# Rotating 96 images by a quarter turn: where the first store stands against the last load

## Chip, cores and metric

The kernel runs on one core of one Trainium2 chip. The metric is the time of one execution on the device, in microseconds (us). The times given are the median of three runs, and one further look with the hardware profiler shows where each engine and the DMA queue spend that time. In the profile PE is TensorE, DVE is VectorE, ACT is ScalarE, POOL is GpSimd, and SP is SyncE, which here does nothing but issue DMAs.

## Reference

```python
def setup_inputs():
    batch, c, h, w = 32, 3, 256, 256
    return {"x": np.random.randn(batch, c, h, w).astype(np.float32)}

def reference(x: np.ndarray) -> np.ndarray:
    return np.rot90(x, k=-1, axes=(-2, -1)).astype(np.float32)
```

There are 32 x 3 = 96 images of 256 x 256 float32 values, 256 KB each. Every image is turned by 90 degrees clockwise. No arithmetic is done: 24 MB are read, rearranged inside each image and 24 MB are written.

## Kernel before

The input is cut into 12 slabs of 8 images, 2 MB each (`n_slabs` is 12, `last` is 11). A slab lies in one SBUF tile `units[n]` of 128 partitions by `I` = 2 halves of `F` = 2048 values, 8 KB per half and partition. All twelve tiles stand in SBUF at once, so no load waits for a tile to come free.

**Loads.** A first loop issues all 24 loads, two for each slab and 1 MB each, on the SP queue. The first and the last slab are loaded as 128 partitions by 8 KB (line 63), the other ten as 64 partitions by 16 KB, on every second partition (line 65).

**Turning.** A second loop over the slabs lets DVE turn one slab with two transposes of 128 x 2048 values (line 73 for the first and the last slab, line 79 for the others). The turned slab n is written into the tile of slab n - 1, which has been read by then. Slab 0 goes to a PSUM tile `turned0`. After the last slab, ACT copies `turned0` into `units[last]` (line 92).

**Stores.** Within the same second loop each turned slab is stored, also from the SP queue. Slab 1 goes out in three parts: 1 KB of each partition (128 KB, line 82), the other 7 KB of that half (896 KB, line 83), and the second half (1 MB, line 84). Slabs 2 and 3 go out in two halves of 1 MB (line 87), slabs 4 to 11 as whole 2 MB transfers (line 89), and slab 0 at the very end (line 93).

**What sets the order.** All 40 transfers are issued by SP in the order of the program, 24 loads and then 16 stores, and they drain one after another through one queue that is spread over 16 DMA engines. The framework hands out eight completion semaphores in turn, so SP issues a transfer only when the one eight places earlier has landed; a store also waits for the transposes that made its data. Stores therefore stand in the queue behind the last loads well before those have landed.

Of the kernel before, what the change touches and what calls it, by code (L numbers as in the profile page):

```python
# [1 line left out]

# [4 lines left out]

@with_exitstack
def kernel(
    ctx: ExitStack,
    tc: tile.TileContext,
    x: bass.AP,
    out: bass.AP,
):

    nc = tc.nc
    fp32 = mybir.dt.float32

    B, C, H, W = x.shape
    P = nc.NUM_PARTITIONS  # L40
    RI, RO = 16, 8
    K = H // RI
    I = 2
    Q = P // (K * I)
    n_slabs = B * C // (Q * I)
    last = n_slabs - 1
    F = RO * W

    rows_in = x.rearrange("b c h w -> (b c h) w")
    rows_out = out.rearrange("b c h w -> (b c h) w")  # L50
    ld8_v = rows_in.rearrange("(n i p r) w -> n p i (r w)", i=I, p=P, r=RO)
    ld16_v = rows_in.rearrange("(n i m r) w -> n i m (r w)", i=I, m=Q * K, r=RI)
    st_v = rows_out.rearrange("(n i p c) w -> n p i (c w)", i=I, p=P, c=RO)

    pools = [ctx.enter_context(tc.tile_pool(name=f"unit{u}", bufs=1)) for u in range(n_slabs)]
    units = [pool.tile([P, I, F], fp32, name=f"u{u}") for u, pool in enumerate(pools)]
    psum = ctx.enter_context(tc.tile_pool(name="psum", bufs=1, space=bass.MemoryType.PSUM))
    turned0 = psum.tile([P, I, F], fp32, name="turned0")

    for n in range(n_slabs):  # L60
        for i in range(I):
            if n in (0, last):
                nc.sync.dma_start(out=units[n][:, i], in_=ld8_v[n][:, i])
            else:
                nc.sync.dma_start(out=units[n][i::I].rearrange("p i f -> p (i f)"), in_=ld16_v[n, i])

    for n in range(n_slabs):
        t_in, t_out = units[n], units[n - 1] if n else turned0
        if n in (0, last):
            for i in range(I):  # L70
                src = t_in[:, i].rearrange("p (r g c) -> p c r g", r=RO, c=RO)
                dst = t_out[:, i].rearrange("p (c g r) -> p c r g", c=RO, r=RO)
                nc.vector.transpose(out=dst[:, :, ::-1, ::-1], in_=src)  # L73
        else:
            src = t_in.rearrange("p i f -> p (i f)").rearrange("p (r g c) -> p c r g", r=RI, c=RO)
            dst = t_out.rearrange("p i (c k r) -> p c r k i", c=RO, r=RI)[:, :, ::-1, ::-1, :]
            for h in range(2):
                cs = slice(h * RO // 2, (h + 1) * RO // 2)
                nc.vector.transpose(out=dst[:, cs], in_=src[:, cs])  # L79

        if n == 1:
            nc.sync.dma_start(out=st_v[n][:, 0, :W], in_=t_out[:, 0, :W])
            nc.sync.dma_start(out=st_v[n][:, 0, W:], in_=t_out[:, 0, W:])
            nc.sync.dma_start(out=st_v[n][:, 1], in_=t_out[:, 1])
        elif n in (2, 3):
            for i in range(I):
                nc.sync.dma_start(out=st_v[n][:, i], in_=t_out[:, i])
        elif n:
            nc.sync.dma_start(out=st_v[n], in_=t_out)

    for i in range(I):
        nc.scalar.copy(out=units[last][:, i], in_=turned0[:, i])  # L92
    nc.sync.dma_start(out=st_v[0], in_=units[last])


# [1 line left out]
_INS = ['x']  # L97
_OUTS = [((32, 3, 256, 256), 'float32')]


# [23 lines left out]
```

## Time and profile before

| | |
|---|---|
| Time, median of three runs | 123.94 us (123.78 to 124.06) |
| The profiled execution's own time | 124.06 us |
| Its span in the profile | 122.3 us |
| DVE busy | 93.3 us, 76% of the span, 24 transposes |
| ACT busy | 5.0 us |
| Moved by DMA | 50.33 MB, 25.17 read and 25.17 written, 412 GB/s over the span |
| DMA packets' time | 97.8% of 16 engines' span |

The span is the part of the execution that the profile covers; the 1.8 us by which the execution's own time is longer lie outside of it. A DMA issue on SP is short (a few tenths of a us) and says only when a transfer is put in the queue; "to landing" is the time from there until its completion semaphore is full. The rows of windows give, for a stretch of the span, the busy time of each engine and the rate at which DMA packets moved bytes.

### The profile page before, as it was taken

How to read it: one execution, taken by the hardware profiler on the slowest of the kernel's cores; microseconds unless marked ns; L12 is line 12 of the kernel's file. 1: busy time of each engine (PE TensorE's matmuls, PEld its weight loads, DVE VectorE, ACT ScalarE, POOL GpSimd, SP SyncE). 2: the span in 40 equal slices, each digit the busy share in tenths (PEclk: the TensorE clock that was granted, in tenths of full speed). 3: DMA queues.
4: the chain of work that ended last, by engine and by line, in shares of the span. 5: the costliest groups of instructions: out<-in, count | busy, mean ns of one | idle time of the engine just before them, and what ended most of it. 6: DMA issues, size and time to landing. Idle time of an engine off the chain costs nothing.

```text
span 122.3 us, 138 instructions
## 1 busy us (share of the span) xinstructions
DVE 93.3 (76%) x24; ACT 5.0 (4%) x3; POOL 0.2 (0%) x4
## 2 busy tenths in 40 slices
DVE  0199999999999999999999999999999940000000
ACT  0000000000000000000400000000000641000000
POOL 0000000000000000000000000000000000000000
DMA  3999999999999999999999999999999999999994
GB/s 118 418 450 429 429 429 429 429 429 429 429 429 429 429 429 429 429 429 391 359 413 429 429 429 426 429 421 429 429 429 429 429 429 429 429 429 426 429 429 180
DMA packets 5632, 50.33 MB, mean 412 GB/s; under 512 B 640, under 2 KB 768, under 8 KB 896
## 3 DMA queue, kind: packets, MB, share of 16 engines
q1 hardware_dynamic: 5632, 50.33, 97.8%
HBM read 25.17 MB, written 25.17 MB: 412 GB/s over the span
## 4 chain that ended last, share of the span: by engine, by line
DVE 47%; issue 27%; DMA 4%; DVEq 3%; ACT 2%
DVE u L79 37%; DVE turned L73 6%; DMA u<-in_x_dram 4%; DVE u L73 3%; DVEq L119 3%; ACT u L92 2%
## 5 line engine op out<-in xcount | busy, mean ns | idle before, releaser
L79 DVE STREAM_TRANSPOSE u<-u 128x2048 f32<-128x2048 f32 x20 | 78.0, 3949 | 0.3
L73 DVE STREAM_TRANSPOSE turned<-u 128x2048 f32<-128x2048 f32 x2 | 7.6, 3828 | 5.6 <-DMA u<-in_x_dram 5.6
L73 DVE STREAM_TRANSPOSE u<-u 128x2048 f32<-128x2048 f32 x2 | 7.7, 3953 | 0.0
L92 ACT COPY u<-turned 128x2048 f32<-128x2048 f32 x2 | 3.7, 1866 | 36.5 <-DVE u L73 36.5
L92 ACT ACT_TABLE_LOAD x1 | 1.3, 1283 | 59.7 <-DMA u<-in_x_dram 59.7
L108 POOL MEMSET const-bfloat16-1.0<- 128x1 bf16 x1 | 0.1, 102 | 0.0
L108 POOL MEMSET const-uint8-127<- 128x1 uint8 x1 | 0.1, 102 | 0.0
L108 POOL MEMSET const-float32-0.0<- 128x1 f32 x1 | 0.1, 99 | 0.2 <-issue 0.2
L108 POOL MEMSET const-float32-1.0<- 128x1 f32 x1 | 0.1, 99 | 0.0
## 6 DMA issues: line engine op xcount, KB each, us to landing
u<-in_x_dram SPq DMA_DIRECT2D x24, 1024.0 KB, 19.6
out_dram<-u SPq DMA_DIRECT2D x9, 2048.0 KB, 23.0
out_dram<-u SPq DMA_DIRECT2D x5, 1024.0 KB, 17.7
out_dram<-u SPq DMA_DIRECT2D x1, 896.0 KB, 17.8
out_dram<-u SPq DMA_DIRECT2D x1, 128.0 KB, 18.3
```

What stands on the lines that cost most here:

```text
L73: nc.vector.transpose(out=dst[:, :, ::-1, ::-1], in_=src)
L79: nc.vector.transpose(out=dst[:, cs], in_=src[:, cs])
L92: nc.scalar.copy(out=units[last][:, i], in_=turned0[:, i])
L108: nc = _bacc.Bacc("TRN2", target_bir_lowering=False, num_devices=1)
L119: with _tile.TileContext(nc) as tc:
```

## The change

`M` is 128 / 4 = 32. The last slab is loaded by three transfers in place of two: its first half as before, then 32 partitions of the second half (256 KB, called `near_end`), then the other 96 partitions (768 KB). The first store, 128 KB of slab 1, gets a dependency on `near_end`, so SP does not issue it until `near_end` has landed, and all later stores stand behind it on SP. Slabs 2 and 3 are stored as whole 2 MB transfers, like slabs 4 to 11. The transposes, the copies and the other loads stay as they are. There are 25 loads and 14 stores, 39 transfers in place of 40.

```diff
     F = RO * W
+    M = P // 4
...
     for n in range(n_slabs):
+        if n == last:
+            nc.sync.dma_start(out=units[n][:, 0], in_=ld8_v[n][:, 0])
+            near_end = nc.sync.dma_start(out=units[n][:M, 1], in_=ld8_v[n][:M, 1])
+            nc.sync.dma_start(out=units[n][M:, 1], in_=ld8_v[n][M:, 1])
+            continue
         for i in range(I):
-            if n in (0, last):
+            if n == 0:
                 nc.sync.dma_start(out=units[n][:, i], in_=ld8_v[n][:, i])
             else:
                 nc.sync.dma_start(out=units[n][i::I].rearrange("p i f -> p (i f)"), in_=ld16_v[n, i])
...
         if n == 1:
-            nc.sync.dma_start(out=st_v[n][:, 0, :W], in_=t_out[:, 0, :W])
+            first = nc.sync.dma_start(out=st_v[n][:, 0, :W], in_=t_out[:, 0, :W])
+            tc.add_manual_dep(first.ins, near_end.ins.name, mybir.DependencyInfo(
+                mybir.DependencyClass.Sync, mybir.DependencyReason.DATA), reason="stores after loads")
             nc.sync.dma_start(out=st_v[n][:, 0, W:], in_=t_out[:, 0, W:])
             nc.sync.dma_start(out=st_v[n][:, 1], in_=t_out[:, 1])
-        elif n in (2, 3):
-            for i in range(I):
-                nc.sync.dma_start(out=st_v[n][:, i], in_=t_out[:, i])
         elif n:
             nc.sync.dma_start(out=st_v[n], in_=t_out)
```

In the changed file the three loads of the last slab are lines 64 to 66, the three stores of slab 1 lines 89, 92 and 93, the whole stores line 95 and the final store line 99.

## Prediction

> **What bounds the kernel now.** I read the page first, its busy times and its 40 slices:
>
> ```profile
> DVE 93.3 (76%) x24; ACT 5.0 (4%) x3; POOL 0.2 (0%) x4
> GB/s 118 418 450 429 429 429 429 429 429 429 429 429 429 429 429 429 429 429 391 359 413 429 429 429 426 429 421 429 429 429 429 429 429 429 429 429 426 429 429 180
> q1 hardware_dynamic: 5632, 50.33, 97.8%
> ```
>
> The DMA engines are occupied for 97.8% of the span and hold 429 GB/s in nearly every slice. Only the ends and slices 19 to 21, about 55 to 64 us, fall below. That middle dip is where the queue passes from loads to stores, and it is all that this change can reach. I next cut the neighbourhood into windows of 2.45 us, which is the time of one 1 MB transfer (1048.6 KB at 428 GB/s). Columns: window; busy time of DVE, ACT and POOL; clock; DMA share; GB/s.
>
> ```profile
> 53.86:56.31 2.45, 2.45 (x2) 0.00 (x0) 0.00 (x0) 1.00 0.99 421
> 56.31:58.76 2.45, 2.45 (x2) 0.00 (x0) 0.00 (x0) 1.00 0.99 418
> 58.76:61.21 2.45, 2.42 (x2) 1.28 (x1) 0.00 (x0) 1.00 0.99 321
> 61.21:63.66 2.45, 2.45 (x1) 0.00 (x0) 0.00 (x0) 1.00 1.01 410
> 63.66:66.11 2.45, 2.45 (x2) 0.00 (x0) 0.00 (x0) 1.00 1.00 422
> ```
>
> The dip is one window deep: at 321 GB/s it lost 107/428 x 2.45 = 0.61 us, while the DMA share stayed at 0.99. So the engines did not stand idle; they moved packets slowly. The packet records say which: the third to fifth of the eight 8 KB packets that each engine moves for the last load took up to 690 ns, most of them over 400, where 309 ns is usual. No store packet began before 61.35 us. So the last load is slow while stores wait behind it.
>
> Third, the timeline of SP, which tells when transfers are put in the queue:
>
> ```profile
> 39.91 2.78 SPq L63 DMA_DIRECT2D u<-in_x_dram  x2
> 44.87 0.35 SPq L82 DMA_DIRECT2D out_dram<-u  x1
> 47.39 0.34 SPq L83 DMA_DIRECT2D out_dram<-u  x1
> 49.81 0.33 SPq L84 DMA_DIRECT2D out_dram<-u  x1
> ```
>
> The first store is queued at 44.87, some 18 us before it lands. Landings come from these issues plus their times to landing (19.7 and 20.3 us for L63's pair, 18.3 for L82, 17.8 for L83): the last load but one lands at 59.62, the last at 62.61, the first store (128 KB) at 63.21, the second (896 KB) at 65.15. Fourth, the only place where the queue starts empty, the beginning, where the first load is issued at 0.73:
>
> ```profile
> 1.00:1.75 0.75, 0.00 (x0) 0.00 (x0) 0.00 (x0) 1.00 0.00 0
> 1.75:2.50 0.75, 0.00 (x0) 0.00 (x0) 0.00 (x0) 1.00 0.66 197
> 2.50:3.25 0.75, 0.00 (x0) 0.00 (x0) 0.00 (x0) 1.00 0.94 360
> 3.25:4.00 0.75, 0.00 (x0) 0.00 (x0) 0.00 (x0) 1.00 1.08 459
> ```
>
> By 4.00, (197 + 360 + 459) x 0.75 = 762 KB have moved, 1.78 us of work at 428 GB/s. The stream thus began as if at full rate at 2.22, **1.49 us after the issue**. The first load lands at 5.62, so landing follows the last byte by 5.62 - 2.22 - 2.45 = 0.95 us. Last, the end:
>
> ```profile
> 120.00:120.75 0.75, 0.00 (x0) 0.00 (x0) 0.00 (x0) 1.00 0.68 284
> 120.75:121.50 0.75, 0.00 (x0) 0.00 (x0) 0.00 (x0) 1.00 0.06 22
> 99.38 1.87 ACT L92 COPY u<-turned 128x2048 f32<-128x2048 f32 x1 [1.92 <-DVE u L73]
> 101.27 0.37 SPq L93 DMA_DIRECT2D out_dram<-u  x1
> ```
>
> Full-rate data ends at 120.0 + 306 x 0.75 / 428 = 120.54. The stores are 24 MB, 24 x 2.45 = 58.8 us, so their stream **began as if at full rate at 61.74**. This is the number to compare with. The last store is queued at 101.27 and its data is not due before about 115.6: compute has some 14 us of cover. A measurement of this kernel can tell about 0.2%, 0.25 us, from no change.
>
> **The change, part by part.**
>
> *The first store moves behind `near_end`.* The last load but one has its last byte at 59.62 - 0.95 = 58.67, and `near_end`, a quarter of 2.45 us, lands at 59.62 + 0.61 = 60.23 if it runs at full rate. SP issues about 0.02 us after a landing (a load that waited for the one of 42.33 was issued at 42.35), so at 60.25. From there an empty queue's 1.49 us run: store data begins as if at full rate at 61.74. The cover is the 768 KB still to load, 1.83 us: loads that are not slowed end at 58.67 + 2.45 = 61.12. The queue would idle for 0.62 us, about what the slow packets cost before. The slow packets go and an empty queue comes in their place; on this part the sum is 0.00.
>
> *The price of 1.49 us* is the disputed one, since it is the start of a load at the head of the program, and no store here starts on an empty queue. It can't be under one issue (0.35 us), which would put the start under the loads' end: then the loads decide at 61.12, a gain of 0.62. At the other end, the packet records show eight of the 16 engines starting at 1.76 and eight at 2.57, 1.84 us after the issue, their slowest first packets 556 ns against 309: 1.84 + 0.25 = 2.09 us, a loss of 0.60. I take 1.49, the one start that the trace has.
>
> *The stores queued behind the first.* All 14 stores stand behind the wait on SP; nothing but the end of the kernel waits for them, as no tile is written again after its store. But the first store has only 128 KB, 0.31 us, to cover the next one's start. At the beginning the second load was issued 0.44 us after the first; on that spacing the second store starts at 60.25 + 0.44 + 1.49 = 62.18, and the first one's data is through at 61.74 + 0.31 = 62.05. Loss **0.13 us**. The 2.14 us of the second store cover the third. The other issues then follow quickly, since their slabs have been turned: DVE ends slab 6 at 60.2 and needs 7.8 us a slab, against 4.9 us for a store, but slab n is due at 61.9 + 4.9 x (n - 1), which for n = 7 is 91 against 68 and for the last 116 against 101.
>
> *`near_end` and the other 96 partitions.* No row has a transfer to 32 neighbouring partitions. The nearest are the loads of line 65, on 64 alternate partitions, which land 2.45 us apart as those of 128 do: no extra cost. The slowest first packet of the beginning, 679 ns, bounds it above: two packets per engine at 679 in place of 309 make 0.74 us, and all of it delays the issue. Below nothing is excluded, since 309 ns is every engine's usual pace. I lean to the nearest row and put in about a quarter of the bound, **0.17 us**. The 96-partition load costs nothing up to 0.62 us of delay; that idle time hides it. Slowed as the old last load was (0.54 us), it would still be hidden.
>
> [...]
>
> *Slabs 2 and 3 as whole stores, 39 transfers in place of 40.* Two 1 MB stores land 2.43 to 2.47 us apart, a 2 MB store every 4.90: nothing either way.
>
> **Sum.** 0.00 + 0.13 + 0.17 = +0.30 us on the profiled execution: 124.06 + 0.30 = 124.36, its span going from 122.3 to 122.6 with the 1.8 us outside unchanged. That execution lies 0.12 above the median, so the median should be about **124.25 us**, 0.25% slower.
>
> **Rivals.**
>
> *Faster: the stores' start is covered.* The dip exists because stores stand behind the last load; if the loads run free and a store, which reads SBUF, starts sooner than a load, only the loads' end counts. For it: the slow packets begin at the third packet of each engine, in both halves of the engines, which start half a us apart; that fits a place in the queue, not a moment. Against it: the start of 1.49 us. It decides below 1.49 - 0.30 = 1.19 us; at 0.87 or less the whole 0.62 is gained with nothing added: 123.32. With a part of it, 123.3 to 123.7.
>
> *Slower still: the cold start is longer, for a quarter transfer that lands late or a first store too small.* For it: the second half of the engines started 0.81 us after the first half, and 0.31 us of data can't cover that. Near the upper bounds, +0.60 for the start, or +0.74 for `near_end` with the 0.13, the time is 124.5 to 125.0.
>
> *It does nothing it says.* If the dip came from the loads' last megabyte itself, `near_end` would lie ahead of it and land on time, and the slow remainder would end at about 61.66, still under the idle time: the main sum stands.
>
> **How the numbers follow.** The main case, a cold start in place of slow packets, from -0.1 to +0.5 us (123.85 to 124.45), has 0.50: 0.17 of it within 0.2% and 0.33 slower. The faster rival has 0.30, all faster. The slower rival has 0.20. That makes 0.30, 0.17 and 0.53. The range goes from 123.4 (0.54 of the 0.62 gained) to 125.05, which leaves out under 2 in 10 between its ends; the likeliest case's own range is 123.85 to 124.45.
>
> **What would show it.** In the changed profile the first store should be issued near 60.25 and not at 44.87. The windows from 58.7 to 61 should show the loads at some 428 GB/s, then one shallow hole near 61.1 to 61.8 with the DMA share well under 1, where before the share stayed at 0.99. The second store should land near 65.3, against 65.15. Issue after 60.4 would mean that `near_end` was slow. No hole, and a second store by 64.8, would show the faster rival. I am wrong altogether if the stores' later spacing leaves 4.90 us, or if a wait of SP on DVE ends last after 70 us.

## The result, and the profile after

The changed kernel takes 125.80 us (median of 6 runs, 125.41 to 126.25) against 123.97 us (median of 6 runs), a ratio of 1.0152 (95% interval 1.0127 to 1.0178). The forecast of a loss had the right sign and missed its size: 1.8 us in place of 0.3, above the range's end of 125.05.

The page of the changed kernel, its rate in 40 slices and its DMA queue:

```profile
GB/s 90 427 453 427 427 437 432 421 437 432 421 432 432 427 427 427 442 421 395 219 357 428 429 416 429 413 424 419 421 416 421 421 421 419 421 421 421 421 421 213
q1 hardware_dynamic: 5616, 50.33, 98.1%
```

Two things differ from before. The dip of slices 19 to 21 has become deep, 219 where 359 was the lowest. And the second half of the span, all stores, runs mostly at 413 to 424, where before it held 429. The queue is still occupied for 98.1% of the span: the loss is slow packets, not idle engines. The windows of 2.45 us at the passage say the same (last two columns: DMA share and GB/s):

```profile
53.86:56.31 2.45, 2.45 (x1) 0.00 (x0) 0.00 (x0) 1.00 0.96 408
56.31:58.76 2.45, 2.45 (x2) 0.00 (x0) 0.00 (x0) 1.00 1.00 418
58.76:61.21 2.45, 2.42 (x2) 1.02 (x1) 0.00 (x0) 1.00 1.04 221
61.21:63.66 2.45, 2.45 (x1) 0.26 (x1) 0.00 (x0) 1.00 0.98 270
63.66:66.11 2.45, 2.45 (x2) 0.00 (x0) 0.00 (x0) 1.00 1.03 426
```

Two windows at 221 and 270, with a share of 1.04 and 0.98: no hole, the engines crawl. The timeline of SP, when the last two loads and the first store are issued:

```profile
42.46 0.35 SPq L65 DMA_DIRECT2D u<-in_x_dram  x1
44.91 0.32 SPq L66 DMA_DIRECT2D u<-in_x_dram  x1
61.84 0.37 SPq L89 DMA_DIRECT2D out_dram<-u  x1
```

And from the page, the DMA issues of `near_end` and of the first store (KB each, us from issue to landing):

```profile
u<-in_x_dram SPq DMA_DIRECT2D x1, 256.0 KB, 19.3
...
out_dram<-u SPq DMA_DIRECT2D x1, 128.0 KB, 2.9
```

`near_end` lands at 42.46 + 19.3, exactly 61.75, where 60.23 was expected, and the first store is issued at 61.84. Its packet records show 8 KB packets of 600 to 760 ns, and of some 430 to 550 ns for the 96 partitions behind it, against the usual 309.

Where the time of this profiled execution went (126.25 us, against 124.06 before, 2.19 more; it is the longest of its six runs): the first load landed 0.12 us later; from there to the second store's landing (66.72 against 65.15) 1.45 us were lost at the passage; from there to the last landing (56.87 us against 56.31) 0.56 us in the pace of the stores; 0.06 us after it.

### The profile page after: what moved, and what is told of

The parts are those of the page before. It is cut to its first block, busy times and chain, and to the rows that moved or that the text cites. A ratio compares the mean times of both kernels' runs of the same rounds, so it can differ in the third digit from the quotient of the medians.

```text
span 124.5 us, 137 instructions
## 1 busy us (share of the span) xinstructions
DVE 93.3 (75%) x24; ACT 5.0 (4%) x3; POOL 0.2 (0%) x4
## 3 DMA queue, kind: packets, MB, share of 16 engines
q1 hardware_dynamic: 5616, 50.33, 98.1%
## 4 chain that ended last, share of the span: by engine, by line
DMA 51%; DVE 13%; issue 10%; DVEq 6%; ACT 1%
DMA u<-in_x_dram 51%; DVE u L86 13%; DVEq L125 6%; ACT u L98 1%; DVE u L80 0%
## 6 DMA issues: line engine op xcount, KB each, us to landing
u<-in_x_dram SPq DMA_DIRECT2D x1, 256.0 KB, 19.3
```

## The experiments

Three questions were open: what makes the split load slow, what the wait costs without it, and why the stores' pace fell. Ratios are to the kernel before on the same chip.

### What makes the split load slow

**The split alone, no wait.**

```diff
             nc.sync.dma_start(out=units[n][:, 0], in_=ld8_v[n][:, 0])
-            nc.sync.dma_start(out=units[n][:, 1], in_=ld8_v[n][:, 1])
+            nc.sync.dma_start(out=units[n][:M, 1], in_=ld8_v[n][:M, 1])
+            nc.sync.dma_start(out=units[n][M:, 1], in_=ld8_v[n][M:, 1])
```

> The kernel before with one part of the change alone: the last megabyte loaded as 32 partitions and 96 partitions, no wait ahead of the first store, slabs 2 and 3 in halves. Theory F (the form: a transfer to a block of neighbouring partitions is slow by itself): the two pieces land as late as in the changed kernel, the second at 64.0 to 64.3 in place of 62.6, and the time is 125.2 to 125.6. Theory W (the wait costs: the queue runs empty and starts cold): the time is that of before, 123.8 to 124.2. Theory T (loads near the end are slow whatever their form, and a split only moves that): last load at 62.6 to 63.0, time under 124.4.

Measured: 125.14 us, ratio 1.0115 (1.0098 to 1.0133). `near_end` landed at 61.04, the other 96 partitions at 63.95, 2.90 us later, and the stores then kept 4.89 us for 2 MB. Theory F holds: 1.39 us, most of the loss of 1.83, needs no wait at all.

**Every fourth partition in place of 32 neighbours, with the wait.**

```diff
-            near_end = nc.sync.dma_start(out=units[n][:M, 1], in_=ld8_v[n][:M, 1])
-            nc.sync.dma_start(out=units[n][M:, 1], in_=ld8_v[n][M:, 1])
+            near_end = nc.sync.dma_start(out=units[n][0::4, 1], in_=ld8_v[n][0::4, 1])
+            for j in range(1, 4):
+                nc.sync.dma_start(out=units[n][j::4, 1], in_=ld8_v[n][j::4, 1])
```

> The changed kernel with the last megabyte in four transfers of 32 partitions each, every fourth partition (0, 4, 8 and so on first), the first store waiting for the first of them. Theory F in the sense of the block of neighbours: the first quarter lands at 60.2 to 60.4 and the time is 124.0 to 124.4. If instead few partitions are slow wherever they lie, the first quarter lands past 61 and the time is 125 to 126. Theory W: 125.4 or more.

Measured: 124.58 us, ratio 1.0070 (1.0054 to 1.0085). The four quarters landed 0.61 to 0.63 us apart, the first at 60.21: 32 partitions are as quick as 128 when they are spread. The second store landed at 64.64. The time is still above the expected 124.4, which the third question explains.

**Neighbours in HBM or neighbours in SBUF.** In the edit above both the HBM rows and the SBUF partitions are spread. Two kernels part them (the first of the four transfers is shown, the other three follow the same pattern); both permute rows of the last slab, so that only their time is read.

```diff
# together in HBM, spread in SBUF
+            near_end = nc.sync.dma_start(out=units[n][0::4, 1], in_=ld8_v[n][0:32, 1])
...
# spread in HBM, together in SBUF
+            near_end = nc.sync.dma_start(out=units[n][0:32, 1], in_=ld8_v[n][0::4, 1])
...
```

> As e3_wait_strided32, but each of the four transfers reads 256 KB that lie together in HBM (rows of partitions 0 to 31, then 32 to 63 and so on) and writes them to every fourth partition. The rows of the last slab's second half thus stand in other places, so the image values of that slab are permuted; its time is read alone. Theory S (the block of neighbouring SBUF partitions is what made the split load slow): the quarter lands at 60.2 to 60.4 as in e3, time 124.4 to 124.8. Theory M (the neighbouring rows in HBM): the quarter lands after 61, time over 125.

> The other half of that test: each of the four transfers reads every fourth 8 KB row and writes a block of 32 neighbouring partitions; the last slab's rows are again permuted and only the time is read. Theory S: every quarter takes about 1.2 us in place of 0.61, the last load lands near 64.3, time over 125.5. Theory M: the quarters land 0.61 to 0.63 apart as in e3, time 124.4 to 124.8.

Measured: together in HBM 124.62 us, 1.0075 (1.0055 to 1.0094); together in SBUF 125.67 us, 1.0162 (1.0144 to 1.0180). The instructions of the first quarter's line, first in the one and then in the other kernel:

```profile
DMA to landing us min/median/max: 17.8/17.8/17.8
```

```profile
DMA to landing us min/median/max: 18.9/18.9/18.9
```

Issued at 42.36 and 42.27, the quarters land at 60.13 and 61.12. With blocks in SBUF the four steps are 1.27, 1.22, 1.16 and 1.14 us, with blocks in HBM 0.62 to 0.63. With the two runs before, all four pairings of block and spread are measured, and only the SBUF side decides. So it is the block of neighbouring SBUF partitions. By these steps 256 KB went into a block at 206 to 230 GB/s and to every fourth partition at 416 to 423, about twice as fast; the windows 58.76:61.21 and 61.21:63.66 of the run with blocks in SBUF show 221 and 201 GB/s, at DMA shares of 1.05 and 0.94. What in the hardware makes a block slow, no run shows. One thing more stands in the run with blocks in SBUF: although the first store waited there too, the stores behind it kept their full rate. The third question comes back to these two windows of it:

```profile
66.00:80.00 14.00, 13.93 (x5) 0.00 (x0) 0.00 (x0) 1.00 1.01 429
90.00:114.00 24.00, 9.18 (x3) 3.73 (x2) 0.00 (x0) 1.00 1.01 427
```

### What the wait costs

**The wait alone, on a transfer of the usual form.**

```diff
-            nc.sync.dma_start(out=units[n][:, 0], in_=ld8_v[n][:, 0])
-            near_end = nc.sync.dma_start(out=units[n][:M, 1], in_=ld8_v[n][:M, 1])
-            nc.sync.dma_start(out=units[n][M:, 1], in_=ld8_v[n][M:, 1])
+            near_end = nc.sync.dma_start(out=units[n][:, 0], in_=ld8_v[n][:, 0])
+            nc.sync.dma_start(out=units[n][:, 1], in_=ld8_v[n][:, 1])
```

> The wait alone, on a transfer of the usual form: the last slab in two loads of 128 partitions as before, the first store waiting for the first of them, so that 1 MB is still to load; slabs 2 and 3 as whole stores. The store is issued near 59.65, an empty queue's 1.49 us end at 61.13, where undisturbed loads end too. Theory F: no idle time and no slow packets, 123.4 to 123.8. Theory W: over 124.3. If the slow packets of the last load come back although no store is queued, 123.9 to 124.2.

Measured: 124.19 us, ratio 1.0043 (1.0026 to 1.0061). Windows of this kernel, two at the passage and one long one among the stores:

```profile
58.76:61.21 2.45, 2.42 (x2) 1.28 (x1) 0.00 (x0) 1.00 0.98 409
61.21:63.66 2.45, 2.45 (x1) 0.00 (x0) 0.00 (x0) 1.00 1.05 424
...
90.00:114.00 24.00, 9.22 (x3) 3.73 (x2) 0.00 (x0) 1.00 1.01 421
```

The dip is gone, 409 where before had 321, and slab 1 was stored by 66.96 in place of 67.58. This execution was already 0.15 us ahead when its last load but one landed, so the passage itself gained 0.47 us, most of the 0.6 us that the faster rival promised. But the eleven slabs after it took 54.70 us against 53.88: the long window runs at 421, where the kernel before has this:

```profile
90.00:114.00 24.00, 9.31 (x3) 3.73 (x2) 0.00 (x0) 1.00 1.01 429
```

A gain of 0.47 at the passage is turned into a loss by a pace that is up to 2% lower. It sets in gradually: of the whole stores the first two landed 4.88 and 4.90 us after the one ahead, those from the fourth on 4.98 to 5.02.

**The same 256 KB cut along the free axis.**

```diff
-            near_end = nc.sync.dma_start(out=units[n][:M, 1], in_=ld8_v[n][:M, 1])
-            nc.sync.dma_start(out=units[n][M:, 1], in_=ld8_v[n][M:, 1])
+            near_end = nc.sync.dma_start(out=units[n][:, 1, :F // 4], in_=ld8_v[n][:, 1, :F // 4])
+            nc.sync.dma_start(out=units[n][:, 1, F // 4:], in_=ld8_v[n][:, 1, F // 4:])
```

> The changed kernel with the same 256 KB and 768 KB, but cut along the free axis: 2 KB and then 6 KB of all 128 partitions. Wait and whole stores stay. Theory F: the 256 KB land at 60.2 to 60.3, the first store is issued at once, the second lands near 65.3, and the time is 124.0 to 124.3, as the sum of the prediction without its 0.17. Theory W: the time stays at 125.4 to 126. If the cold start is shorter than the 1.49 us taken, 123.4 to 123.9.

Measured: 125.35 us, ratio 1.0139 (1.0117 to 1.0162), a miss. The quarter in 2 KB rows needed 1.02 us, not 0.61. The second store landed at 64.96, earlier than before, and then the pace was 5.01 us for 2 MB. Theory W came nearest to the time, but not for the reason that it named: the queue had hardly a hole (its windows at the passage have DMA shares of 0.98 and 1.00).

### Why the stores' pace fell

In the changed kernel and the first three runs with a wait on another form of transfer, the 2 MB stores landed 4.95 to 5.01 us apart on average, and their 8 KB packets took 314 to 316 ns (means after 67 us); without a wait, 4.90 us and 309 ns. The two groups also differed in how slabs 2 and 3 were stored, so that was parted first.

**Whole stores without a wait; halves with a wait.**

```diff
# the first: taken out of the kernel before
-        elif n in (2, 3):
-            for i in range(I):
-                nc.sync.dma_start(out=st_v[n][:, i], in_=t_out[:, i])
# the second: the same three lines put into the kernel of the wait alone
```

> The kernel before with one part of the change alone: slabs 2 and 3 stored whole, no wait and no split load. In the four runs with the wait, 2 MB stores landed 4.98 to 5.00 us apart and their 8 KB packets took 314 to 315 ns; without it (and with halves) 4.90 us and 309 ns. Theory R (the pace is set by how the stores start: queued behind loads they run at 309 ns, started after the loads at 315 ns): pace 4.90, time 123.5 to 123.9, as before. Theory H (the pace is set by the early whole stores): pace 4.98 to 5.00, time 124.4 to 124.8.

> The wait on the first half of the last slab (as in e4_wait_half), and slabs 2 and 3 stored in halves again. Theory R: pace 4.98 to 5.00 as in e4, time 124.0 to 124.4. Theory H: pace 4.90, and what e4 gained until slab 1 was stored (66.97 against 67.58) stays: 123.1 to 123.4.

Measured: whole stores without a wait 123.85 us, 1.0016 (1.0007 to 1.0025); halves with the wait 124.19 us, 1.0041 (1.0025 to 1.0056). The long window, of the first and then of the second:

```profile
90.00:114.00 24.00, 9.18 (x3) 3.73 (x2) 0.00 (x0) 1.00 1.01 429
```

```profile
90.00:114.00 24.00, 9.34 (x3) 3.73 (x2) 0.00 (x0) 1.00 1.01 420
```

Theory H falls, and of the two theory R is left: the pace goes with the wait, and the size of two early stores costs some 0.2%.

**The wait placed earlier: 2 MB or 1.5 MB still to load.**

```diff
# 2 MB left: near_end is the last load of the slab before the last;
# the last slab is loaded by two transfers of 1 MB, as in the kernel before
-                nc.sync.dma_start(out=units[n][i::I].rearrange("p i f -> p (i f)"), in_=ld16_v[n, i])
+                near_end = nc.sync.dma_start(out=units[n][i::I].rearrange("p i f -> p (i f)"), in_=ld16_v[n, i])
# 1.5 MB left: the first megabyte of the last slab in two
+            near_end = nc.sync.dma_start(out=units[n][0::2, 0], in_=ld8_v[n][0::2, 0])
+            nc.sync.dma_start(out=units[n][1::2, 0], in_=ld8_v[n][1::2, 0])
+            nc.sync.dma_start(out=units[n][:, 1], in_=ld8_v[n][:, 1])
```

> The wait moved to the second load of the slab before the last, so 2 MB are still to load when the first store is issued near 57.0. Theory R: the stores stand behind loads for some 4 us, so the slow packets in the last load return, and with them the pace of 4.90; time as before, 123.4 to 123.9. If the wait itself spoils the pace: pace 4.98 to 5.00, time 124.2 or more.

> The wait on half of the last slab's first megabyte, cut into two transfers on alternate partitions, so that 1.5 MB are left at the issue near 58.4. Between e4 (1 MB left: no slow packets, slow pace) and e10. Theory R: the slow packets return in part or whole, and the pace lies at 4.90 to 4.95; time 123.4 to 124.1. If pace and slow packets are independent, this could have both at their best: 122.9 to 123.2.

Measured: 2 MB left 123.56 us, ratio 0.9978 (0.9965 to 0.9990); 1.5 MB left 123.49 us, 0.9966 (0.9953 to 0.9979). With 2 MB left:

```profile
58.76:61.21 2.45, 2.42 (x2) 1.28 (x1) 0.00 (x0) 1.00 1.01 408
...
90.00:114.00 24.00, 9.29 (x3) 3.73 (x2) 0.00 (x0) 1.00 1.01 428
```

Both now beat the kernel before, by 0.2 and 0.3%. The pace is back at 4.89 us, as theory R wants, but its other half missed with 2 MB left: the last load landed 2.49 us after the one ahead of it, not some 2.9, although stores stood queued behind it for 4 us (with 1.5 MB left it was 2.63 us). So a store behind the last load is not enough to slow it.

**The size of the first store.** The kernel before, with slab 1 as one 2 MB store (the three lines of slab 1 taken out).

> The kernel before with slab 1 stored as one 2 MB transfer in place of 128 KB, 896 KB and 1 MB; no wait, usual loads. If the 1 KB packets of the first store cause the slow packets of the last load, these go and the time is 122.9 to 123.3. If it is enough that any store is queued behind: slow packets as before, 123.5 to 123.9.

Measured: 124.03 us, ratio 1.0014 (1.0002 to 1.0026). The last load was as slow as before (2.98 us after the one ahead of it), so the 1 KB packets don't cause it.

**An empty queue.** The first try made only the first store wait for the last load.

```diff
-            near_end = nc.sync.dma_start(out=units[n][:, 0], in_=ld8_v[n][:, 0])
-            nc.sync.dma_start(out=units[n][:, 1], in_=ld8_v[n][:, 1])
+            nc.sync.dma_start(out=units[n][:, 0], in_=ld8_v[n][:, 0])
+            near_end = nc.sync.dma_start(out=units[n][:, 1], in_=ld8_v[n][:, 1])
```

> As e4_wait_half, but the first store waits for the very last load, so the queue is empty when it is issued. Last load near 62.0, first store issued at once. The prediction's start of 1.49 us puts its landing 2.75 us after the issue (64.7) and the second store's near 66.9, 2.3 later than in e4; time 126.2 to 126.6. If an empty queue starts faster, as the 2.33 to 2.41 us from issue to landing in the runs with 0.75 MB left suggest, the second store lands near 66.3 and the time is 125.6 to 126. Theory R (stores issued too late to be read ahead keep a slow pace): 4.98 to 5.00 us for 2 MB. If the pace is 4.90, theory R falls.

Measured: 124.99 us, ratio 1.0085 (1.0062 to 1.0109). It did not measure an empty queue: in the order that the framework chose, SP issued the 896 KB store at 44.79, ahead of the waiting one, and that store covered the gap. The pace was 5.00 us all the same, though a store had stood behind the loads. So theory R in its first wording, "queued behind loads", was too narrow. Two more kernels made all later stores wait, once at the passage and once between two stores.

```diff
# at the passage: near_end is the very last load, slab 1 is one store
+        if n:
+            st = nc.sync.dma_start(out=st_v[n], in_=t_out)
+            tc.add_manual_dep(st.ins, near_end.ins.name, ...)
...
# among the stores of the kernel before, also ahead of the final store
+            st = nc.sync.dma_start(out=st_v[n], in_=t_out)
+            if n == 4:
+                fourth = st
+            if n > 4:
+                tc.add_manual_dep(st.ins, fourth.ins.name, ...)
...
```

> All stores wait for the very last load, slab 1 is stored as one 2 MB transfer, so the queue is empty when the first store is issued, near 62.0. By the prediction's 1.49 us the first 2 MB land 4.90 + 2.44 = 7.34 us after the issue (69.3); if an empty queue starts a store in 1.0 to 1.1 us, as the runs with 0.75 MB left suggest, 6.9 to 7.0 us after. Theory R (a queue that ran empty leaves a slow pace): 4.98 to 5.00 us per 2 MB afterwards, time 126.0 to 126.6; otherwise 4.90 and 125.0 to 125.6.

> The kernel before, with every store from slab 5 on waiting until slab 4's store has landed (near 82.3). The queue runs empty among the stores alone; the passage from loads to stores is as before. Issue to landing of slab 5's store as in e13: 7.3 us by the prediction's start, 6.9 to 7.0 by the shorter one, in place of 4.9 behind a full queue. If running empty is what leaves the slow pace, slabs 6 and later land 4.98 to 5.00 us apart, before that 4.90; time 126.3 to 127. If the slow pace belongs to the passage from loads to stores, 4.90 throughout and 125.7 to 126.4.

Measured: emptied at the passage 126.42 us, 1.0219 (1.0202 to 1.0236); emptied among the stores 126.02 us, 1.0192 (1.0177 to 1.0207). The windows of the second, where slab 5's store is issued at 81.88:

```profile
81.00:81.50 0.50, 0.50 (x1) 0.00 (x0) 0.00 (x0) 1.00 0.29 115
81.50:82.00 0.50, 0.50 (x1) 0.00 (x0) 0.00 (x0) 1.00 0.00 0
82.00:82.50 0.50, 0.50 (x1) 0.00 (x0) 0.00 (x0) 1.00 0.00 0
82.50:83.00 0.50, 0.50 (x1) 0.00 (x0) 0.00 (x0) 1.00 0.63 262
```

And two long windows of it, ahead of the hole and after it:

```profile
66.00:80.00 14.00, 13.93 (x5) 0.00 (x0) 0.00 (x0) 1.00 1.01 428
...
90.00:114.00 24.00, 9.27 (x3) 3.73 (x2) 0.00 (x0) 1.00 1.01 420
```

Here is a real hole, 1.3 us by the packet records (81.47 to 82.77), and no load has a part in it: the stores ran at 428 before it and at 420 ever after, 4.90 and then some 5.0 us for 2 MB. The time of 126.02 us alone would not tell, as it lies in the range expected for a pace of 4.90; the spacing decides, and the start was shorter than expected. In the other kernel the stores after the hole also landed 5.0 us apart. In both, the 16 engines had their first packet 0.9 to 1.1 us after the issue (from 63.01 on for 62.09, from 82.77 on for 81.88), and the 2 MB landed 6.6 us after it, not the 7.34 that the prediction's start gives.

## Why the prediction was right or wrong

**Sign and place** were right, the sign in part by luck. All of the change happens at the passage and after it; compute stays hidden, and SP's order did what the diff says. But the forecast of a loss rested on two small terms: the 0.13, which did not come, and the 0.17, which was only a part of a bound. With the wait on a transfer of the usual form the passage gained time.

**`near_end`, 0.17 us: the step that failed.** The delay was 1.52 us (61.75 against 60.23; 0.12 of it is the later start of the whole execution), twice the upper bound of 0.74. That bound took the slowest first packet of the beginning, 679 ns, for the slowest possible; here they took up to 760. The issue at 61.84, past 60.4, is the sign that I had named for a slow `near_end`. I took the loads on 64 alternate partitions as the nearest row, but in the quality that matters, spread or block, that row is the opposite of this transfer: spread partitions ran at full rate and blocks at half (0.62 against 1.14 to 1.27 us). The delay has a second part: the load ahead of `near_end` also landed late, 2.98 us after its forerunner in place of 2.49, in the changed kernel and by less in the split alone (2.79). Why a transfer slows the tail of the one ahead of it was not settled.

**The 96 partitions at no cost: wrong.** They landed 2.55 us after `near_end`, where 1.83 was due. The idle time that should have hidden them did not exist: in the packet records at least 16 packets are under way at every moment from 57 to 70 us.

**The start of 1.49 us and the 0.13 of the second store: too long.** An empty queue landed 2 MB in 6.6 us, 0.7 us less than 1.49 gives, and the lag of half the engines at the head of the program did not come back. With a quick quarter the second store landed at 64.64 and 64.57, against the 65.3 of my sum. The "faster" rival was thus right about the passage: with the wait on a usual transfer 0.47 of the 0.6 us came.

**The pace of the stores: missing from the sum.** I wrote that I would be wrong altogether if the spacing left 4.90 us. It did: 4.86 at first, then up to 5.06 in the changed kernel, 0.56 us of its loss, and in the wait alone it cost 0.8 us and reversed the gain. No row of before could show it, since its first stores stood in the queue some 17 us before the loads had ended.

**What the experiments show and leave open.** Shown: a queue that runs empty among stores leaves a pace about 2% lower (e14). An empty queue is not needed for it: in the changed kernel and in both runs with the wait on half of the last slab (e4, e6), at least 16 packets are under way throughout the passage, and the pace fell all the same. What orders all the runs with a wait is the time for which the queue still had work when the first waiting store was issued. Taking the last byte 0.95 us ahead of its landing, this was 3.9 us with 2 MB left (e10), 2.8 with 1.5 MB left (e11) and 2.5 with blocks in SBUF (e9, where only 0.75 MB were left, but slow ones): the pace stayed at 4.89. It was 1.5 us in the changed kernel and 1.4 or less in the others: the pace fell. By this order the limit lies between 1.5 and 2.5 us, and it goes by time, not by bytes; no run was made to test the order by itself.

Why the packets become slower is not known. In the kernel before, every 8 KB packet after 70 us took 309 ns; with the wait on half of the last slab 74% of them did so between 70 and 80 us and 19% between 90 and 114, most others 2 to 10 ns more. Nor was the cause of the slow packets in the kernel before found: they lose most of their size with a wait 1.5 or 2 MB ahead (the last load 2.63 and 2.49 us after the one ahead of it, against 2.99), and with slab 1 stored as one transfer of 2 MB they stayed (2.98).

## What to carry to other kernels

Cut a small transfer so that its SBUF partitions are spread (every fourth one), not into a block of 32 neighbours: here the loads of the last 1 MB in four blocks landed 2.6 us later than in four spread quarters (64.64 against 62.00). The whole kernel differs by 1.05 us only (125.67 against 124.62), because behind the blocks the stores kept the full pace. When a wait is put ahead of queued transfers, leave the queue clearly more work than one issue needs to start (here 2.5 us of it was enough and 1.5 us was not), and read the pace of everything behind the wait, not only the place of the wait. When the nearest row differs from the new operation in one property, ask whether that property is the one that counts before you take its price.

## What was not expected of the hardware

- After the queue had run empty among the stores, they kept a lower pace until the end: 8 KB packets of 316 ns on average for 309, 420 GB/s for 428, over the remaining 40 us and more; loads that started on an empty queue at the head of the program showed no such loss (2.44 to 2.46 us per megabyte for the 16 loads after the first).
- A 256 KB load to 32 neighbouring partitions took 1.14 to 1.27 us, to every fourth partition 0.61 to 0.63 us, with its rows in HBM spread or together.
- A 256 KB load in rows of 2 KB took 1.02 us in place of 0.61.
- The first 2 MB store from an empty queue landed 6.6 us after its issue, at the passage and among the stores alike; behind a full queue, in the kernel before, such stores landed 4.89 to 4.91 us apart.
